# A two-layer encoder on one core: the Toeplitz blocks of the state-space branch recorded per half, and DMA prices of the list scheduler changed

## The chip, the cores and the metric

The kernel runs on one core of a Trainium2 chip. The metric is the device time of one execution in microseconds (us), lower is better. The engines are TensorE (PE in the rows; PEld is its weight load), VectorE (DVE), ScalarE (ACT), GpSimd (POOL) and SyncE (SP). SP does nothing but issue DMAs; POOL issues some too. Line L745 is the one line of the scheduler's `emit` through which every instruction of the kernel before is issued (L751 after the change), so all rows carry it, and work is told apart by the names of its tiles.

## The reference

Two layers over x of 256 tokens by 1024 channels, all float32:

```
for l in range(2):
    mod = silu(c) @ w_ada[l] + b_ada[l]            # shift, scale, gate, twice
    h = layer_norm(x) * (1 + scale1) + shift1
    proj = h @ w_in[l]                             # all branches and three gates
    o_mla = latent_attention(...); o_ret = retention(...); o_s5 = s5(s5_u, ...)
    merged = sig(g0)*(o_mla @ w0) + sig(g1)*(o_ret @ w1) + sig(g2)*(o_s5 @ w2)
    x = post_norm(ALPHA * x + gate1 * (merged @ w_o[l]))
    h = layer_norm(x) * (1 + scale2) + shift2
    x = post_norm(ALPHA * x + gate2 * conv_ffn(h))
```

The part that the change touches is `s5`: 32 groups of 16 channels, each with a complex diagonal recurrence of 64 states, run forward and backward over the tokens, whose outputs are added; then a gelu and a gated 512x512 product.

## The kernel before

**Weights.** Each weight block of 128x1024 (512 KB) is loaded as `raw` by SP, cast by ACT to a rounded `hi`, and VectorE forms `lo` = raw - hi. Every large product is three matmuls (hi by hi, lo by hi, hi by lo). Some blocks come through POOL's DMAs instead (`hd`, `ld`). The adaptive-norm weights `ada` and `adab` are loaded by SP in blocks of the same size.

**The state-space branch.** The 256 tokens are cut into 32 blocks of 8. What reaches a block from other blocks goes through the states: `U` and `w1` give `St`, scaled sums of these give `X`, and matmuls `Y<-w,X` bring it to the output. What the 8 tokens of a block do to one another is the direct term: a Toeplitz matrix of 8x8 blocks of 16x16 channels. Its 15 different blocks, 240 columns, are computed as `kps` (matmuls of `bbt` by `w`), and ACT and VectorE write them to the tile `R`, one tile for m = 0, 1 and one for m = 2, 3 (m counts four slices of the channels; the two tiles are called half 1 and half 2 here). To lay them out as a matrix, each half goes to DRAM (`rd<-R`, 4 DMAs) and comes back eight times, each time 16 columns further on (`T<-rd`, 16 DMAs of 64 KB a half, 8 for each of its two tiles `T`). Then 8 matmuls `Y<-T,U` for each m add the direct term to `Y`. Behind `Y` follow gelu, `zF`, the gated product `glu_ps`, the branch's output product `br_ps`, the output projection `wo_acc`, and the residual sum and norm (`y`, `xn`, h), before the first matmul `upt` of the feed-forward part.

**Order.** No instruction is issued where it is written. All go to a `Recorder` with their dependences, their place in the program as priority (with a small jitter), and a duration from `cost()`. `schedule()` then simulates the five engines: each free engine takes the ready instruction of best priority whose tiles find a place (tiles lie in pools of fixed size; the pool `k4` has 37 places of 4 KB a partition, and holds `raw`, `hi`, `lo`, `R` and `T`). Each engine executes the order that comes out, in that order. A DMA also waits until the one issued eight earlier by the same engine has landed. Work that may fill waits is recorded between the steps of a branch by `filler(n)`: products of the gates (`g_ps`) and of the other branches (`br_ps`), and gate weights.

**Names and lines.** `Pool` is at line 387, the duration of a DMA at 507 to 509, the transfer model of `schedule()` at 690 to 692, the loop over m of the direct term from 1754, `filler(F_S5)` at 1777, and the DRAM round trip at 1778 to 1785. In `cost()` a DMA of SP keeps its queue for 600 ns and lands 2000 ns and its bytes later, one of POOL 1100 and 2500. The round trip of both halves is recorded after the loop over m, so its priority is behind all four m and their fillers.

Of the kernel before, what the change touches and what calls it, by code (L numbers as in the profile page):

```python
# [10 lines left out]
F32 = mybir.dt.float32  # L11
# [10 lines left out]
P = 128  # L22
# [363 lines left out]

class Pool:
    def __init__(self, rec, real, bufs, psum):
        self.rec, self.real, self.bufs, self.psum = rec, real, bufs, psum

    def tile(self, shape, dt, tag=None, name=None):
        s = Slot(self.rec, self, shape, dt, tag, name)
# [22 lines left out]
class Recorder:  # L415
# [79 lines left out]
    @staticmethod  # L495
    def cost(eng, method, outs, ins, kw):
        n = max([r.free() for r in outs + ins] or [1])
        psum = any(r.tile_.pool.psum for r in outs + ins)
        if eng == "PE":
            if method == "transpose":  # L500
                return 109, 60
            n, m = kw["rhs"].free(), kw["lhsT"].free()
            if kw["rhs"].tile_.dt == F32R:
                return max(107, n / 2.4) + 13.5, 60
            t = 4 * max(n, 16) / 2.4
            return (t / 4 + 22 if m <= 32 else max(t, 4 * m / 2.4) / 2 + m / 2.4 if m <= 64 else max(t, 4 * m / 2.4) + 4), 60
        if method == "dma_start":
            by = [r for r in outs + ins]
            return (1100 if eng == "POOL" else 600), (2500 if eng == "POOL" else 2000) + sum(r.idx.shape[0] * 16 * r.free() * 4 for r in by) / 360
        if eng == "ACT":  # L510
            aps = sum(isinstance(kw.get(k), Ref) for k in ("scale", "bias"))
            return (65 if psum else 100) + 0.82 * n + 88 * aps + (93 if "accum_out" in kw else 0), 90
        aps = sum(isinstance(kw.get(k), Ref) for k in ("scalar", "scalar1", "scalar2"))
        if eng == "POOL":
            if method == "memset":
                return 60 + 0.3 * n, 90
            if kw.get("op") == ALU.pow:
                return 300 + 165 * n, 90
            if method == "tensor_scalar":
                return 175 + (0.6 if kw.get("op1") else 3.36) * n, 90  # L520
            if n < 300:
                return 200 + 1.8 * n, 90
            few = any(0 in z for r in ins for z in [np.diff(r.idx[0].ravel()[:2])])
            return 148 + (1.67 if few else 2.1) * n, 90
        if method == "tensor_tensor_scan":
            return 68 + 2.07 * n, 90
        if method == "transpose":
            return 80 + 1.94 * n, 90
        if method in ("tensor_copy", "tensor_scalar", "memset") and not psum:
            return 66 + 0.53 * n + 60 * aps, 90  # L530
        return 68 + 1.042 * n + 60 * aps, 90
# [31 lines left out]
    def schedule(self):  # L563
# [14 lines left out]
        for k, v in self.tags.items():  # L578
# [4 lines left out]
            if need[k].max(initial=0) > self.bufs[k]:  # L583
                i = int(need[k].argmax())
# [50 lines left out]
        while done < len(ops):  # L635
            progress = True
            while progress:
                progress = False
                for e in names:
# [48 lines left out]
                            ticks[k] = ticks.get(k, 0.0) + o.cols * max(0.0, min(b, k + 1) - max(a, k)) / (b - a)  # L688
                    busy[e] = now + dur
                    if o.method == "dma_start":  # L690
                        dma_free = max(dma_free, now + o.dur) + (o.lat - (2500 if e == "POOL" else 2000))
                        o.end = dma_free + (2500 if e == "POOL" else 2000)
                    else:
                        o.end = now + dur
                    heapq.heappush(events, (busy[e], -1))
# [53 lines left out]
def build(tc, A, dbg=None):  # L749
# [4 lines left out]
    def pool(name, bufs, **kw):  # L754
        return Pool(rec, ctx.enter_context(tc.tile_pool(name=name, bufs=1, **kw)), bufs, kw.get("space") == PSUM)

    cp = pool("const", 1)
    drp = pool("dram", 1, space=DRAM)
    k4 = pool("k4", N4)
    k2 = pool("k2", N2)  # L760
    k1 = pool("k1", N1)
# [16 lines left out]
    def bank(shape, name):  # L778
        return psp.tile(shape, F32, tag="ps", name=name)
# [638 lines left out]
    def mixer(l, xt, h, s5, xdram, ready=None, pre_=None):  # L1418
# [330 lines left out]

        R = [t4([P, 2, 2, 240], "R") for _ in range(2)]  # L1750
        Y = [bank([P, 4, P], "Y") for _ in range(2)]
        for m in range(4):
            w2 = [s5.gen(m, d, "w2") for d in range(2)]
            kps = [bank([P, 2, P], f"kps{g}") for g in range(2)]
# [14 lines left out]
            for d in range(2):  # L1769
                for r in range(2):  # L1770
                    with rec.group():
                        for g in range(2):
                            for qq in range(4):
                                mm(out=Y[g][32 * qq:32 * qq + 32, m], lhsT=X[d][grp[g], r, m * 4 + qq],
                                   rhs=w2[d][grp[g], r, qq].rearrange("p a b -> p (a b)"),
                                   start=(m == 0 and d == 0 and r == 0), stop=False)
            filler(F_S5)
        Tt = [t4([P, 4, 2, P], "T") for _ in range(4)]
        for mh_ in range(2):
            rd = drp.tile([16, 4, 4, 240], F32, name=f"rd{l}{mh_}")  # L1780
            for qq in range(4):
                SY.dma_start(out=rd[:, qq], in_=R[mh_][32 * qq:32 * qq + 16].rearrange("p m g x -> p (m g) x"))
            for m, i in ((m, i) for m in range(2) for i in range(8)):
                SY.dma_start(out=Tt[2 * mh_ + m][16 * i:16 * i + 16],
                             in_=rd[:, :, 2 * m:2 * m + 2, (7 - i) * 16:(7 - i) * 16 + P])
        for m in range(4):
            with rec.group():
                for g, qq in ((g, qq) for g in range(2) for qq in range(4)):
# [191 lines left out]
```

## Time and profile before

| | before |
|---|---|
| time, median of 3 runs | 1040.67 us (1039.1 to 1042.18) |
| profiled execution, its own time | 1044.28 us |
| its span | 1042.5 us |
| TensorE busy | 968.3 us (93%) |
| VectorE busy | 839.1 us (80%) |
| ScalarE busy | 516.2 us (50%) |
| GpSimd busy | 84.1 us (8%) |
| DMA | 232.98 MB, 223 GB/s on average |
| mean granted clock of TensorE | 0.984 |

The profiled execution has 1.8 us outside its span and is 3.6 us above the median of the runs. TensorE is busy in 93% of the span, so time can only be won in its 74 us of idle time or where it ran at the lower of its two clock levels. The chain of waits that ended last lies on TensorE for 69%, on VectorE for 15% and on DMAs for 7%; `T<-rd` is 2% of it.

### The profile page before, as it was taken

How to read it: one execution, taken by the hardware profiler on the slowest of the kernel's cores; microseconds unless marked ns; L12 is line 12 of the kernel's file. 1: busy time of each engine (PE TensorE's matmuls, PEld its weight loads, DVE VectorE, ACT ScalarE, POOL GpSimd, SP SyncE). 2: the span in 40 equal slices, each digit the busy share in tenths (PEclk: the TensorE clock that was granted, in tenths of full speed). 3: DMA queues.
4: the chain of work that ended last, by engine and by line, in shares of the span. 5: the costliest groups of instructions: out<-in, count | busy, mean ns of one | idle time of the engine just before them, and what ended most of it. 6: DMA issues, size and time to landing. Idle time of an engine off the chain costs nothing.

```text
span 1042.5 us, 21330 instructions
## 1 busy us (share of the span) xinstructions
PE 968.3 (93%) x8470; PEld 849.1 (81%) x8470; DVE 839.1 (80%) x1659; ACT 516.2 (50%) x895; POOL 84.1 (8%) x115
## 2 busy tenths in 40 slices
PE   4899998888998999999989999998799979999995
PEld 3689877678986799999957988687698869999994
DVE  8999998944499996777898788899266999777766
ACT  2357464224464565555635556532246466555640
POOL 0022123000002000000012010130000010000001
PEclk9999999999999999999999999999999999999998
DMA  9988589697975975555559563796898466555601
GB/s 352 408 342 183 162 220 266 153 235 249 393 269 197 355 279 196 183 189 175 184 215 396 180 170 115 175 245 149 219 388 297 145 222 206 199 182 183 221 2 41
DMA packets 72499, 232.98 MB, mean 223 GB/s; under 512 B 8384, under 2 KB 16592, under 8 KB 72400
## 3 DMA queue, kind: packets, MB, share of 16 engines
q1 hardware_dynamic: 62032, 193.88, 52.6%
q0 software_dynamic: 10368, 37.75, 15.2%
q8 instruction: 66, 1.08, 0.4%
q14 instruction: 33, 0.27, 0.1%
HBM read 228.50 MB, written 3.10 MB: 222 GB/s over the span
## 4 chain that ended last, share of the span: by engine, by line
PE 69%; DVE 15%; DMA 7%; issue 3%; ACT 2%; SPq 2%; POOL 1%; POOLq 0%; DVEq 0%; ACTq 0%
PE up_ps L745 22%; PE dn_acc L745 11%; PE g_ps L745 8%; PE b L745 6%; DVE g L745 3%; PE br_ps L745 3%; PE upt L745 3%; DMA T<-rd 2%; PE ada_ps L745 2%; SPq L745 2%; PE u_ps L745 2%; DMA raw<-in_wts 2%; PE wo_acc L745 2%; DMA hd<-in_wts 2%; DVE lo L745 2%
## 5 line engine op out<-in xcount | busy, mean ns | idle before, releaser
L745 DVE TENSOR_TENSOR lo<-raw,hi 128x1024 fp32r<-128x1024 f32 (+1 forms) x210 | 252.4, 1216 | 72.6 <-ACT hi L745 25.9
L745 ACT CAST hi<-raw 128x1024 fp32r<-128x1024 f32 (+1 forms) x210 | 214.1, 1041 | 76.1 <-DMA raw<-in_wts 27.5
L745 PE MATMUL up_ps<-hh,hi 128*128 128x256 f32 x640 | 181.2, 283 | 0.0
L745 PE MATMUL up_ps<-hlo,hi 128*128 128x256 f32 x640 | 181.1, 283 | 0.0
L745 PE MATMUL up_ps<-hh,lo 128*128 128x256 f32 x640 | 181.0, 283 | 0.0
L745 PEld LDWEIGHTS up_ps<-hh,hi 128*128 128x128 f32 x640 | 122.7, 192 | 2.5 <-issue 1.2
L745 PEld LDWEIGHTS up_ps<-hlo,hi 128*128 128x128 f32 x640 | 122.7, 192 | 1.6 <-issue 0.4
L745 PEld LDWEIGHTS up_ps<-hh,lo 128*128 128x128 f32 x640 | 122.7, 192 | 0.1
L745 DVE SCALAR_TENSOR_TENSOR cv<-up_ps,small,cv 128x255 f32<-128x255 f32 x176 | 73.0, 477 | 14.8 <-ACT cv L745 14.8
L745 PE MATMUL g_ps<-hh,hd 128*128 128x256 f32 x256 | 77.2, 301 | 1.0 <-ACT pe L745 1.0
L745 PE MATMUL g_ps<-hlo,hd 128*128 128x256 f32 x256 | 74.6, 292 | 0.0
L745 PE MATMUL g_ps<-hh,ld 128*128 128x256 f32 x256 | 74.2, 290 | 0.0
L745 PE MATMUL dn_acc<-lo,ah 128*128 128x512 f32 x176 | 68.4, 392 | 0.0
L745 PE MATMUL dn_acc<-hi,ah 128*128 128x512 f32 x176 | 66.7, 392 | 0.0
L745 PE MATMUL dn_acc<-hi,al 128*128 128x512 f32 x176 | 66.3, 390 | 0.0
L745 ACT ACTIVATE cv<-up_ps,small 128x256 f32<-128x256 f32 x88 | 44.6, 561 | 34.5 <-PE up_ps L745 34.3
L745 ACT ACTIVATE gt<-g_ps 128x256 f32<-128x256 f32 x48 | 18.2, 382 | 79.6 <-PE g_ps L745 79.6
L745 ACT ACTIVATE ld<-hd 128x1024 fp32r<-128x1024 f32 x36 | 37.9, 1062 | 35.2 <-DMA hd<-in_wts 24.2
L745 PEld LDWEIGHTS g_ps<-hh,hd 128*128 128x128 f32 x256 | 49.8, 195 | 5.8 <-issue 3.7
L745 PEld LDWEIGHTS g_ps<-hh,ld 128*128 128x128 f32 x256 | 49.8, 195 | 1.2 <-issue 1.1
L745 PEld LDWEIGHTS g_ps<-hlo,hd 128*128 128x128 f32 x256 | 49.8, 194 | 1.2 <-issue 0.8
L745 ACT CAST hl<-raw 128x512 fp32r<-128x512 f32 x48 | 29.0, 620 | 42.6 <-PE br_ps L745 12.2
(332 smaller groups left out, 2329.9 us busy)
## 6 DMA issues: line engine op xcount, KB each, us to landing
raw<-in_wts SPq DMA_DIRECT2D x226, 512.0 KB, 4.9
ada<-in_wts SPq DMA_DIRECT2D x48, 512.0 KB, 8.9
adab<-in_wts SPq DMA_DIRECT2D x48, 512.0 KB, 10.2
hd<-in_wts POOLq DMA_DIRECT2D x36, 512.0 KB, 6.8
ld<-in_wts POOLq DMA_DIRECT2D x36, 512.0 KB, 7.8
T<-rd SPq DMA_DIRECT2D x64, 64.0 KB, 4.6
lnrow<-in_rows SPq DMA_DIRECT2D x8, 512.0 KB, 8.7
raw<-in_wts SPq DMA_DIRECT2D x8, 416.0 KB
```

What stands on the lines that cost most here:

```text
L745: getattr(o.eng.real, method)(*a, **kw)
```

## The change

The DRAM round trip becomes a function, `toeplitz`, which is recorded inside the loop over m, for half 1 after m = 1 and for half 2 after m = 3, each ahead of that m's filler; so it gets an earlier priority. The `T` tiles are asked for there, too. And `cost()` prices DMAs anew: POOL 800 ns of queue and 4500 ns and the bytes; SP where it reads a DRAM tile of the program's own 620 and 4600 without bytes; every other DMA of SP 380 and 2000 and the bytes. The prices are used only by the scheduler's simulation.

```diff
 class Pool:
     def __init__(self, rec, real, bufs, psum):
-        self.rec, self.real, self.bufs, self.psum = rec, real, bufs, psum
+        self.rec, self.real, self.bufs, self.psum, self.dram = rec, real, bufs, psum, False
...
         if method == "dma_start":
-            by = [r for r in outs + ins]
-            return (1100 if eng == "POOL" else 600), (2500 if eng == "POOL" else 2000) + sum(r.idx.shape[0] * 16 * r.free() * 4 for r in by) / 360
+
+            by = sum(r.idx.shape[0] * 16 * r.free() * 4 for r in outs + ins) / 360
+            if eng == "POOL":
+                return 800, 4500 + by
+            if any(r.tile_.pool.dram for r in ins):
+                return 620, 4600
+            return 380, 2000 + by
...
                     if o.method == "dma_start":
-                        dma_free = max(dma_free, now + o.dur) + (o.lat - (2500 if e == "POOL" else 2000))
-                        o.end = dma_free + (2500 if e == "POOL" else 2000)
+                        fix = 4500 if e == "POOL" else 4600 if o.lat == 4600 else 2000
+                        dma_free = max(dma_free, now + o.dur) + (o.lat - fix)
+                        o.end = dma_free + fix
...
+    drp.dram = True
...
+        Tt = []
+
+        def toeplitz(mh_):
+
+            rd = drp.tile([16, 4, 4, 240], F32, name=f"rd{l}{mh_}")
+            for qq in range(4):
+                SY.dma_start(out=rd[:, qq], in_=R[mh_][32 * qq:32 * qq + 16].rearrange("p m g x -> p (m g) x"))
+            for m in range(2):
+                Tt.append(t4([P, 4, 2, P], "T"))
+                for i in range(8):
+                    SY.dma_start(out=Tt[-1][16 * i:16 * i + 16], in_=rd[:, :, 2 * m:2 * m + 2, (7 - i) * 16:(7 - i) * 16 + P])
+
         for m in range(4):
...
+            if m % 2:
+                toeplitz(m // 2)
             filler(F_S5)
-        Tt = [t4([P, 4, 2, P], "T") for _ in range(4)]
-        for mh_ in range(2):
...
```

No engine gets more or other work, but for one copy that goes from ACT to VectorE (1659 and 1660 instructions on VectorE, 854 and 853 in the order of ACT). The order changes on every engine and over the whole program, since every load has a new price. Three places follow.

The first is SP's queue in layer 1, around the two round trips; `rd_8684` is half 1, `rd_8982` (after the change `rd_9024`) half 2. Before:

```order
L745 DMA rd_8684<-R 16x960 x4
L745 DMA T<-rd_8684 16x8x128 x16
L745 DMA rd_8982<-R 16x960 x4
L745 DMA ada<-in_wts 128x1024 x2
L745 DMA raw<-in_wts 128x1024 x2
L745 DMA T<-rd_8982 16x8x128 x16
```

and after the change:

```order
L751 DMA rd_8684<-R 16x960 x4
L751 DMA T<-rd_8684 16x8x128 x16
L751 DMA rows<-in_rows 128x1024
L751 DMA raw<-in_wts 128x1024 x2
L751 DMA rd_9024<-R 16x960 x4
L751 DMA raw<-in_wts 128x1024 x3
L751 DMA adab<-in_wts 128x1024 x3
L751 DMA T<-rd_9024 16x8x128 x16
```

Three loads moved between half 1's return and half 2's way out, and six instead of four stand ahead of half 2's return. In layer 0 five loads (three `ada`, two `raw`) stand in the first gap, where there was none, and four (three `raw`, one `rows`) in the second, where there were five. On TensorE, where in layer 0 three matmuls stood between the `Y<-T,U` of m = 0 and of m = 1, the two now stand back to back, with 47 matmuls of fillers between the last `kps` and the first of them (39 before), and 31 between the third and fourth (16 before). In layer 1, 132 matmuls stand between the second and the third (73 before).

The second place is VectorE's queue in the front of layer 0, ahead of the rotated keys `kr` (whose branch, like `uT` behind it, TensorE's order waits for there). Before:

```order
L745 SCALAR_TENSOR_TENSOR gtmp<-gtmp 128x16
L745 TENSOR_TENSOR lo<-raw,hi 128x1024
L745 CAST hh<-hf 128x2x128
L745 TENSOR_TENSOR hlo<-hf,hh 128x2x128
L745 TENSOR_TENSOR lo<-raw,hi 128x1024
L745 TENSOR_SCALAR ve<-ss 128x1
L745 TENSOR_TENSOR rot_85<-g_799,g_808 128x32x16
L745 TENSOR_SCALAR ve<-ss 128x1
L745 TENSOR_TENSOR kr<-b_310,cst 128x16
```

and after the change:

```order
L751 CAST hh<-hf 128x2x128
L751 SCALAR_TENSOR_TENSOR gtmp<-gtmp 128x16
L751 TENSOR_TENSOR hlo<-hf,hh 128x2x128
L751 SCALAR_TENSOR_TENSOR lg<-gtmp 128x16
L751 CAST hh<-hf 128x2x128
L751 TENSOR_SCALAR nlg<-lg 128x16
L751 TENSOR_TENSOR hlo<-hf,hh 128x2x128
L751 TENSOR_TENSOR w_899<-g_853,g_867 128x512
L751 TENSOR_TENSOR g_904<-pw,bbt 128x512
L751 TENSOR_TENSOR lo<-raw,hi 128x1024
L751 TENSOR_SCALAR ve<-ss 128x1 x2
L751 TENSOR_TENSOR kr<-b_312,cst 128x16
```

In all, 16 more instructions stand ahead of `kr` (278 instead of 262): ten small ones of the retention decays (`gtmp`, `lg`, `nlg`), four products `g<-pw,bbt`, one `w` and one `lo`; ahead of `uT` it is 17 more. On TensorE 33 `g_ps` matmuls that stood among those of `w_ps` and `St` right behind this place now come later.

The third place is VectorE's queue at the end of layer 0's mixer, where the residual sum `y` starts the norm on which the feed-forward part waits. Before:

```order
L745 TENSOR_TENSOR lo<-raw,hi 128x1024
L745 TENSOR_TENSOR bbt<-g_3938,g_3945 128x32x16
L745 TENSOR_TENSOR lo<-raw,hi 128x1024
L745 TENSOR_TENSOR g_4128<-rot_4111,rot_538 128x32
L745 TENSOR_TENSOR y<-wo_acc,rows 128x512 x2
L745 TENSOR_TENSOR y<-y,xa 128x512
```

and after the change:

```order
L751 TENSOR_TENSOR g_4173<-rot_3981,rot_540 128x32x4
L751 TENSOR_TENSOR rot_4051<-g_4173,g_4178 128x32x4
L751 TENSOR_TENSOR g_4194<-rot_4051,rot_540 128x32x8
L751 TENSOR_TENSOR rot_3981<-g_4188,g_4194 128x32x8
L751 TENSOR_TENSOR y<-wo_acc,rows 128x512 x2
L751 TENSOR_TENSOR g_4188<-rot_3981,rot_540 128x32x8
L751 TENSOR_TENSOR y<-y,xa 128x512
```

Twenty small products of the next layer's rotation tables (`rot`, `g`), which stood behind `y`, now stand ahead of it.

## Rows read from the trace of the kernel before

**Rows 1.** Waits of TensorE: us in total, times, longest.

```profile
PE Y L745 <- DMA T<-rd: 10.3, 5, 3.0
...
PE Y L745 <- issue: 1.6, 1, 1.6
```

**Rows 2.** Timeline of TensorE, direct term, layer 0: start, length, idle before.

```profile
222.66 0.64 PE L745 MATMUL Y<-T,U 128*32 128x128 f32 x16
...
226.84 0.65 PE L745 MATMUL Y<-T,U 128*32 128x128 f32 x16 [2.99 <-DMA T<-rd]
...
246.91 0.65 PE L745 MATMUL Y<-T,U 128*32 128x128 f32 x16 [1.71 <-DMA T<-rd]
```

**Rows 3.** Timeline of TensorE, direct term, layer 1.

```profile
733.47 0.64 PE L745 MATMUL Y<-T,U 128*32 128x128 f32 x16 [1.35 <-DMA T<-rd]
...
746.96 0.65 PE L745 MATMUL Y<-T,U 128*32 128x128 f32 x16 [2.03 <-DMA T<-rd]
...
752.27 0.64 PE L745 MATMUL Y<-T,U 128*32 128x128 f32 x16 [2.20 <-DMA T<-rd]
```

**Rows 4.** Windows: length, then busy time of PE, PEld, DVE, ACT, POOL; clock; DMA.

```profile
227.70:231.10 3.40, 3.40 (x18) 3.40 (x18) 0.00 (x0) 0.00 (x0) 0.00 (x0) 0.50 0.88 300
753.40:756.80 3.40, 3.40 (x18) 3.40 (x17) 2.25 (x3) 3.40 (x6) 0.00 (x0) 0.50 1.03 414
```

**Rows 5.** Timeline of SP's DMA issues, layer 0: start, stretch, count.

```profile
202.35 1.73 SPq L745 DMA_DIRECT2D rd<-R  x4
207.61 14.73 SPq L745 DMA_DIRECT2D T<-rd  x16
222.45 2.04 SPq L745 DMA_DIRECT2D rd<-R  x4
...
226.49 1.78 SPq L745 DMA_DIRECT2D raw<-in_wts  x4
228.49 16.38 SPq L745 DMA_DIRECT2D T<-rd  x16
```

**Rows 6.** Waits of SP's queue, 205 to 246 us.

```profile
SPq L745 <- DMA raw<-in_wts: 5.0, 4, 1.7
...
SPq L745 <- DVE g L745: 2.4, 1, 2.4
```

**Rows 7.** Timeline of SP's DMA issues, layer 1.

```profile
730.50 3.38 SPq L745 DMA_DIRECT2D rd<-R  x4
...
737.46 12.72 SPq L745 DMA_DIRECT2D T<-rd  x16
```

**Rows 8.** Timeline of VectorE, the writes that complete the two halves of R, layer 0.

```profile
201.99 0.30 DVE L745 TENSOR_TENSOR R<-R,kps 128x16 f32<-128x16 f32 x2
...
219.28 0.17 DVE L745 TENSOR_TENSOR R<-R,kps 128x16 f32<-128x16 f32 x1
```

**Rows 9.** Windows of four stages, columns as in rows 4.

```profile
50.00:105.00 55.00, 54.76 (x481) 47.77 (x479) 52.74 (x118) 35.37 (x65) 11.76 (x17) 1.00 0.85 264
165.00:219.00 54.00, 46.26 (x797) 37.92 (x796) 50.47 (x118) 17.05 (x39) 9.78 (x13) 1.00 0.77 195
322.00:338.00 16.00, 12.44 (x105) 8.96 (x104) 15.61 (x30) 7.38 (x14) 5.58 (x5) 0.97 0.71 273
755.00:800.00 45.00, 45.00 (x384) 43.02 (x384) 27.49 (x33) 24.51 (x38) 0.00 (x0) 0.98 0.96 361
```

**Rows 10.** VectorE's work by shape, 21 to 100 us: count, busy, mean ns, idle before.

```profile
L745 DVE TENSOR_TENSOR lo<-raw,hi 128x1024 fp32r<-128x1024 f32 x14 | 16.8, 1221 | 0.3 <-ACT hi L745 0.2
L745 DVE TENSOR_TENSOR g<-pw,bbt 128x512 f32<-128x512 f32 x10 | 6.5, 675 | 0.0
...
L745 DVE SCALAR_TENSOR_TENSOR gtmp<-gtmp 128x16 f32<-128x16 f32 x9 | 1.4, 159 | 0.0
```

**Rows 11.** Timeline of VectorE ahead of layer 0's first residual sum.

```profile
322.00 0.21 DVE L745 TENSOR_TENSOR g<-rot,rot 128x32 f32<-128x32 f32 x1
322.19 1.29 DVE L745 TENSOR_TENSOR y<-wo_acc,rows 128x512 f32<-128x512 f32 x2
```

More of the change, by code (lines that the diff above doesn't have):

```diff
@@ L1776, in mixer @@
                                    start=(m == 0 and d == 0 and r == 0), stop=False)
+            if m % 2:
+                toeplitz(m // 2)
             filler(F_S5)
-        Tt = [t4([P, 4, 2, P], "T") for _ in range(4)]
-        for mh_ in range(2):
[L1780 to L1785, printed above, removed]
         for m in range(4):
```

## The prediction

> **What bounds the kernel now.** I read the busy times first: TensorE works for 968 of 1042.5 us, so its idle time and its stretches at the lower clock are all there is to win, and anything that adds idle time to it is lost. Then the waits of TensorE by tile: for the direct term it waits 10.3 us in five waits for `T<-rd`, and once 1.6 us that end in "issue" [rows 1]. The timeline gives each wait's place: in layer 0 none before m = 0, 2.99 us before m = 1, 1.58 before m = 2 (the issue wait of rows 1) and 1.71 before m = 3 [rows 2]; in layer 1 1.35, 2.03 and 2.20 [rows 3]. That is 6.28 and 5.58 us, together 11.9. Last, the windows: three such waits are followed by a stretch of 3.4 us in which TensorE was busy throughout and the granted clock was 0.50, the 1.2 GHz level; rows 4 show two of the three, the other begins at 248.2. At half clock 3.4 us do 1.7 us of work, so these cost 5.1 us more. All in all 17.0 us hang on the arrival of `T`.
>
> What sets that arrival: half 1 is complete at 202.29 (201.99 and 0.30) [rows 8], and its DMAs to DRAM are issued from 202.35 [rows 5], at once. So the earlier priority can win nothing ahead of half 1. Its sixteen returns then hold SP for 14.7 us (207.61 to 222.34) [rows 5], 2.4 of them in one wait for VectorE to give a place in the pool [rows 6]. Half 2 is complete at 219.45 [rows 8], but goes out from 222.45 [rows 5], 3.0 us late, since the queue is still issuing half 1's returns. In layer 1 it is alike: half 2's way out starts at 730.50 and the return at 737.46 [rows 7].
>
> **The change part by part.** The profiled execution, 1044.28 us, is what the sum is made against; the median of the runs is 3.6 us below it.
>
> *Layer 0, half 1.* The ninth return of half 1 no longer stands behind a tile that VectorE must free, which took 2.4 us [rows 6]; the second `T` lands by so much earlier. On TensorE m = 0 and 1 stand together behind eight more matmuls of filler. Full-clock filler takes 0.12 us a matmul (384 in 45.00 us) [rows 9], so TensorE also comes 1.0 us later, less the three matmuls, 0.36 us, that were between. The wait of 2.99 us thus shrinks by 2.4 at least and vanishes at most: I take -2.4. The stretch at half clock right behind it [rows 4] goes if the pause does: -1.7.
>
> *Layer 0, half 2.* Five loads stand newly ahead of its way out. Four `raw` issue in 1.78 us [rows 5], 0.45 each, so 2.2 us, which eats the 2.4 that half 1 gave; its return stands behind four loads instead of five. I take -0.4 for the one issue fewer; bounds are -3.3 (both waits gone) and +4, for the case that the loads' data hold up the returns: four waits for `raw` cost 5.0 us in this place already [rows 6].
>
> *Layer 1.* TensorE has 59 more matmuls between m = 1 and m = 2 (132 and 73), 49 of which are net over the stretch from half 1 to the last `Y<-T,U`: 5.9 us of cover. Against it half 2's way out stands behind three loads, at 0.45 us 1.3 us, and its return behind two more than before, 0.9 us by their issue and 2.9 by their data (512 KB at 361 GB/s is 1.45 us each) [rows 9]. So of 5.58 us of waits 1.9 to 3.9 should be left; I take 2.5, -3.1, and half a chance that the stretch at half clock from 753.4 [rows 4] goes: -0.9. The filler taken forward is missing after `Y`: TensorE is busy 45.00 of 45 us from 755 to 800 [rows 9], so 5.9 us less there cost nothing while the gelu and the product behind it arrive within the 39 us that are left; if they didn't, up to 5.9 us would come back.
>
> *Front of layer 0.* Ahead of `kr` VectorE gets ten small operations of 0.159 us, five of the 128x512 kind of 0.675 and one `lo` of 1.22 [rows 10]: 6.2 us by their lengths, about 5.1 to 5.7 since one starts before the one ahead ends. From 50 to 105 us TensorE has 0.24 us of idle time, VectorE 2.3 [rows 9]. So TensorE's order, which now has 33 filler matmuls (4.0 us) fewer among `w_ps` and `St`, waits there for `kr` and `uT`. It is not lost in full: the work is only moved, VectorE's queue up to the completion of R is 1 us longer and no more, and TensorE has 7.7 us of idle time from 165 to 219 [rows 9] which the deferred filler can take. Bounds 0 and +5.7; I take +3.0, in the middle, for want of a row that is nearer.
>
> *End of layer 0's mixer.* Twenty small products of 0.21 us, starting 0.19 after one another [rows 11], move ahead of `y`: 4.0 us, less what moves behind it, 2.9 net. `y` started directly behind the operation ahead of it [rows 11], and VectorE is busy 15.61 of 16 us while TensorE waits 3.6 of them [rows 9]. So nothing hides VectorE's work but what `wo_acc` still lacks then; bounds 0 and +2.9; I take +2.0.
>
> *All the rest* (the FFN, the other boundaries, layer 1's front) keeps its order to within some tenths, and I take nothing for it; the copy that goes to VectorE is under 0.7 us on an engine with slack.
>
> The sum: -2.4 - 1.7 - 0.4 - 3.1 - 0.9 + 3.0 + 2.0 = -3.5, so 1040.8 for a profiled execution and 1037.2 on the scale of the median.
>
> One rule speaks against the gain. In the rows SP's waits for `raw` sit in the middle of half 2's returns, four of them [rows 6]: loads issued ahead of small returns do hold them up. The Trainium skill's page "DMA: Bandwidth & Descriptors", section "Queues, rings and completion order", says the same from below: on each DMA engine the descriptors of one issuing engine's row are consumed in ring order. By it, two more loads ahead of the return in layer 1 would cost their full data time (the 2.9 above and not the 0.9), and the sum would be about 2 us worse; the trace agrees in direction and shows no size for it alone.
>
> **The rivals.**
>
> *A. The front of layer 0 decides (slower).* VectorE's 5.7 us ahead of `uT` become 5.7 us of TensorE idle time that nothing gives back, since VectorE paces this part anyway (52.74 of 55 us, 50.47 of 54) [rows 9], and `y` comes 2.9 late; of the gain the 4.1 of layer 0's half 1 remains: +5.7 + 2.9 - 4.1 = +4.5, 1045.2. For it: no idle time there that could hide anything. Against: the idle time from 165 on. It decides once more than 4 of the 8.6 us stay.
>
> *B. The loads eat the gain.* Layer 0's half 1 keeps its 4.1, but half 2 arrives as late as TensorE does, in both layers (no -0.4, -3.1, -0.9): +0.9, 1041.6. For it: five and three loads in the way of half 2, three and six more ahead of returns [rows 6]. Against: the 49 matmuls of cover.
>
> *C. VectorE's moves are absorbed.* Deferred filler takes the idle time from 165 to 219, and `y` waits for `wo_acc` in any case: -8.5, 1032.2. At the far end all 17.0 us go: 1023.7.
>
> *D. Nothing changes for T,* since half 1 was sent at once before [rows 5, 8] and half 2 waits behind the same queue: the waits stay, the two costs are small: 1040.7.
>
> **How the numbers follow.** A measurement of this kernel can tell a change of about 0.3%, 3.1 us. I give the forecast (1033.5 to 1040.5) 0.33, of which 0.23 lies below 1037.5; A 0.24, C 0.20, B 0.14, D 0.09. Faster: 0.23 + 0.20 = 0.43. Same: 0.10 of the forecast, nearly all of B and D and a little of A: 0.31. Slower: 0.22 of A and 0.04 of B, 0.26. The range for 8 in 10 leaves a tenth on each side: below it most of C's far part, above it the full price of A with a stretch at half clock more: 1029 to 1046. The forecast's own range is 1033.5 to 1040.5.
>
> **What would show it.** In layer 0 m = 0 and 1 of `Y<-T,U` stand together with a wait under 0.6 us, and no window at clock 0.50 follows. In layer 1 the waits before `Y<-T,U` add up to 2 to 4 us instead of 5.58. From 50 to 105 us TensorE shows 2 to 6 us of idle time that ends with `kr`, `uT` or `w_ps` and VectorE, and its idle time from 165 to 219 is smaller by about half of that. `y` starts 2 to 3 us later against the end of `wo_acc`. The prediction is wrong if TensorE's idle time changes mainly elsewhere, if half 2's returns land over 4 us later against the completion of R, or if the front keeps its 0.24 us.

## The result, and the profile after

The changed kernel takes 1050.78 us (median of 4 runs, 1049.38 to 1051.92), the one before 1040.72 beside it: a ratio of 1.0085 with an interval of 1.0062 to 1.0109. It is slower by 10 us, where 3.5 us less were forecast, and lies above the stated range. The two profiled executions, which the rest of this section compares, differ by 7.6 us (1051.92 and 1044.28).

The page of the changed kernel, its span, the busy times and the granted clock in 40 slices:

```profile
span 1049.9 us, 21329 instructions
...
PE 974.5 (93%) x8470; PEld 855.7 (81%) x8470; DVE 841.4 (80%) x1660; ACT 517.7 (49%) x894; POOL 84.3 (8%) x115
...
PEclk8989999998999899999999999999899989999998
```

TensorE is busy 974.5 us with the same 8470 matmuls that took 968.3 before: 6.2 us of the 7.4 by which the two spans differ. Its idle time grew by 1.2 us only (75.4 and 74.2). So most of the difference between the two profiles is busy time, which the same matmuls spend where TensorE runs at 1.2 GHz. The waits of TensorE (us in total, times, longest):

```profile
PE Y L751 <- DMA T<-rd: 17.7, 4, 6.0
...
PE ada_ps L751 <- DMA adab<-in_wts: 8.5, 3, 4.7
...
PE h_ps L751 <- DVE gtmp L751: 2.3, 1, 2.3
```

The waits for `T` are 17.7 us and not the forecast 6 [rows 1]; the other two rows had 3.7 us (for `adab`) and nothing of that kind before. On the timeline the `Y<-T,U` stand as the order had them, but wait longer [rows 2, 3]:

```profile
222.93 0.65 PE L751 MATMUL Y<-T,U 128*32 128x128 f32 x16
...
228.04 0.92 PE L751 MATMUL Y<-T,U 128*32 128x128 f32 x16 [4.47 <-DMA T<-rd]
...
248.18 1.08 PE L751 MATMUL Y<-T,U 128*32 128x128 f32 x16 [5.64 <-DMA T<-rd]
...
733.63 0.64 PE L751 MATMUL Y<-T,U 128*32 128x128 f32 x16
...
740.72 1.08 PE L751 MATMUL Y<-T,U 128*32 128x128 f32 x16 [6.01 <-DMA T<-rd]
...
764.95 0.65 PE L751 MATMUL Y<-T,U 128*32 128x128 f32 x16 [1.61 <-DMA T<-rd]
```

In layer 1 the first of them started before the change at

```profile
731.48 0.65 PE L745 MATMUL Y<-T,U 128*32 128x128 f32 x16
```

These starts tell where the time goes, since as many matmuls, to within two, stand ahead of them in both kernels. At the first `Y<-T,U` of layer 0 the changed kernel is 0.3 us behind (222.93 and 222.66); from there to the last `dn_acc`, the end of layer 0's feed-forward part, it loses 4.6 us, wins 2.7 in the front of layer 1, and loses 5.2 us from layer 1's first `Y<-T,U` on. The loss lies behind `Y<-T,U`, in both layers.

At two of these waits, and elsewhere, the windows (columns as in rows 4) show stretches at 0.50 that last 6.8 us, where each was 3.4 [rows 4]. There are seven of 6.8 us in this execution ahead of its end. One of them is at a wait for VectorE's `gtmp` and two are at waits for `T`:

```profile
67.80:74.60 6.80, 6.53 (x25) 5.13 (x18) 5.68 (x20) 3.48 (x10) 0.52 (x1) 0.50 0.32 125
245.30:252.10 6.80, 3.92 (x29) 3.57 (x30) 0.00 (x0) 1.01 (x2) 0.00 (x0) 0.50 0.48 101
736.90:743.70 6.80, 2.98 (x25) 2.63 (x26) 0.00 (x0) 1.06 (x1) 0.84 (x1) 0.50 1.04 322
```

Three others (340.9, 651.5 and 842.7 us) have 3.4 us near their place in the kernel before. The seventh, at 20.1 us, stood there before too: the clock record of that execution begins only at 26.3 us, but the same matmul takes 0.55 us at 21 us in both kernels, before (first line; the second is at full clock) and after (third line). So the mean clock of 0.984 before counts some 6 us at half clock as full.

```profile
21.34 0.55 PE L745 MATMUL b<-lo,hh 128*128 128x416 f32 x1
40.18 0.35 PE L745 MATMUL b<-lo,hh 128*128 128x416 f32 x1
...
21.17 0.55 PE L751 MATMUL b<-lo,hh 128*128 128x416 f32 x1
```

What made `T` late is in SP's issues: layer 0 in full, then half 2 of layer 1 [rows 5, 7]:

```profile
204.68 12.59 SPq L751 DMA_DIRECT2D T<-rd  x16
217.38 2.22 SPq L751 DMA_DIRECT2D ada<-in_wts  x3
219.70 4.47 SPq L751 DMA_DIRECT2D raw<-in_wts  x2
225.52 3.82 SPq L751 DMA_DIRECT2D rd<-R  x4
230.37 5.34 SPq L751 DMA_DIRECT2D raw<-in_wts  x3
236.70 0.33 SPq L751 DMA_DIRECT2D rows<-in_rows  x1
237.40 12.82 SPq L751 DMA_DIRECT2D T<-rd  x16
...
733.04 7.54 SPq L751 DMA_DIRECT2D rd<-R  x4
...
747.75 15.08 SPq L751 DMA_DIRECT2D T<-rd  x16
```

and in VectorE's last write to R, layer 0 and layer 1 [rows 8]:

```profile
219.10 0.29 DVE L751 TENSOR_TENSOR R<-R,kps 128x16 f32<-128x16 f32 x2
...
732.53 0.17 DVE L751 TENSOR_TENSOR R<-R,kps 128x16 f32<-128x16 f32 x1
```

R's half 2 is complete at 219.39, as before, but its way out is issued from 225.52 to 229.34 and its return from 237.40; before it was 222.45 to 224.49 and 228.49. In layer 1 the way out starts 0.3 us behind R (732.70), but takes 7.5 us for four DMAs, and the return starts at 747.75. A DMA of SP waits for the landing of the one issued eight earlier. For the ways out that was mostly not a load but one of half 1's own last returns; so SP's queue waited 6.8 us for `T` in layer 0 (the second `raw` and the first two ways out) and 6.0 in layer 1 (the ways out):

```profile
SPq L751 <- DMA T<-rd: 6.8, 3, 3.7
...
SPq L751 <- DMA T<-rd: 6.0, 2, 4.2
```

Behind the ways out the loads wait for earlier loads, in layer 0 3.0 us for `ada` and 3.0 for `raw` between 230 and 237.4 us, and half 2's return stands behind them. Read off T's 512-byte packets in the trace, half 2 has landed 50.4 and 50.9 us after R's half 1 was complete, 43.9 and 41.3 before.

Half 1's returns, for which the ways out waited, landed late themselves. In layer 0 the last of them was issued at 216.65, 4.0 us earlier than before, and its last packet moved at 227.43, 1.1 us later. In that stretch the DMA engines are busy without a gap, at 256 GB/s (clock, DMA share and GB/s are the last three columns):

```profile
216.65:227.43 10.78, 6.92 (x101) 6.32 (x83) 3.58 (x10) 4.03 (x9) 1.69 (x2) 1.00 1.09 256
```

In it SP issued five loads of 512 KB, of which 1.2 loads' worth of bytes moved, and GpSimd's queue moved 3.4. In layer 1 the last return landed 9.5 us after its issue, beside 2.9 loads' worth from GpSimd and 1.2 from SP; in layer 0 of e10 below, with no load moving, it took 2.0 us. The Trainium skill, page "DMA: Bandwidth & Descriptors", section "Queues, rings and completion order", says that each DMA engine takes turns between the queue rows it has work for, a whole packet from one before the next. The late tail beside GpSimd's loads agrees with that; no run here measures it alone.

The front of layer 0, 50 to 105 us and 165 to 219 us [rows 9]:

```profile
50.00:105.00 55.00, 52.03 (x391) 45.50 (x392) 52.35 (x115) 35.41 (x64) 10.78 (x16) 0.94 0.77 249
165.00:219.00 54.00, 49.79 (x841) 41.62 (x837) 51.27 (x119) 18.14 (x42) 11.07 (x14) 1.00 0.79 198
```

TensorE's idle time there is 2.97 us instead of 0.24, and 4.21 instead of 7.74.

### The profile page after: what moved, and what is told of

Its sections match the earlier page's. It is cut to its first block, busy times and chain, and to the rows that moved or that the text cites. A ratio compares the mean times of both kernels' runs of the same rounds, so it can differ in the third digit from the quotient of the medians.

```text
span 1049.9 us, 21329 instructions
## 1 busy us (share of the span) xinstructions
PE 974.5 (93%) x8470; PEld 855.7 (81%) x8470; DVE 841.4 (80%) x1660; ACT 517.7 (49%) x894; POOL 84.3 (8%) x115
## 5 line engine op out<-in xcount | busy, mean ns | idle before, releaser
L751 PE MATMUL g_ps<-hlo,hd 128*128 128x256 f32 x256 | 74.2, 290 | 0.0
L751 ACT ACTIVATE cv<-up_ps,small 128x256 f32<-128x256 f32 x88 | 44.9, 562 | 30.8 <-PE up_ps L751 30.3
L751 DVE TENSOR_TENSOR hl<-raw,hl 128x512 fp32r<-128x512 f32 x48 | 32.1, 684 | 32.7 <-ACT hl L751 32.5
```

Of the source, the lines that this page charges most:

```text
L751: getattr(o.eng.real, method)(*a, **kw)
```

## The experiments

A short name for each edit: *move* is the round trip recorded inside the loop over m; *SP 380*, *POOL* and *T* are the three new prices. The seed is that of the scheduler's jitter. "Fillers" counts the matmuls that the order puts on TensorE between the `Y<-T,U` of half 1 and the first of half 2, in layer 0 and layer 1, repeats counted (on this count the kernel before has 93 and 84, where the text above counts rows for layer 1). "Waits" is TensorE's time before `Y<-T,U` in the profiled execution, unless VectorE ended it. The ratio is to the kernel before on the same chip.

| kernel | median us | ratio, interval | waits us | fillers |
|---|---|---|---|---|
| before | 1040.7 to 1044.1 | 1 | 11.9 | 93, 84 |
| whole change | 1050.8 | 1.0085, 1.0062 to 1.0109 | 17.7 | 97, 149 |
| e1 move | 1037.7 | 0.9941, 0.9921 to 0.9961 | 7.0 | 151, 160 |
| e2 the three prices, no move | 1051.4 | 1.0076, 1.0048 to 1.0105 | 11.3 | 73, 71 |
| e3 before, seed 18 | 1038.1 | 0.9950, 0.9929 to 0.9972 | 10.3 | 144, 145 |
| e4 whole change, seed 18 | 1052.5 | 1.0091, 1.0066 to 1.0116 | 17.3 | 144, 152 |
| e5 move, SP 380 | 1045.7 | 1.0042, 1.0022 to 1.0061 | 13.3 | 140, 147 |
| e6 move, POOL | 1033.6 | 0.9926, 0.9904 to 0.9947 | 9.6 | 177, 175 |
| e7 move, T | 1049.0 | 1.0066, 1.0035 to 1.0098 | 16.6 | 144, 140 |
| e8 move, POOL, T | 1044.9 | 1.0030, 1.0002 to 1.0058 | 12.4 | 171, 145 |
| e9 whole change, T not behind rd | 1047.2 | 1.0046, 1.0028 to 1.0064 | 16.7 | 97, 149 |
| e10 move, T with bytes | 1029.9 | 0.9880, 0.9851 to 0.9910 | 7.0 | 172, 172 |
| e11 move, T without bytes, 2364 | 1053.0 | 1.0102, 1.0071 to 1.0133 | 17.3 | 127, 124 |
| e12 move, POOL, SP 900 | 1039.7 | 0.9964, 0.9944 to 0.9984 | 3.8 | 100, 109 |
| e13 e10 with Y of half 2 earlier | 1049.6 | 1.0078, 1.0049 to 1.0107 | 16.7 | 127, 124 |
| e14 whole change, T with bytes | 1042.0 | 1.0002, 0.9978 to 1.0026 | 10.9 | 132, 176 |
| e15 move, POOL, T with bytes | 1037.9 | 0.9956, 0.9934 to 0.9977 | 9.1 | 199, 176 |
| e16 e10, seed 18 | 1034.6 | 0.9928, 0.9904 to 0.9952 | 6.7 | 172, 161 |
| e17 e11, seed 18 | 1049.2 | 1.0054, 1.0037 to 1.0071 | 17.7 | 151, 128 |
| e18 e10 with 7000 | 1034.2 | 0.9901, 0.9874 to 0.9929 | 0.7 | 192, 201 |

Every kernel with more than 12 us of these waits is slower than the one before, every one with less than 10.5 is faster; between them lie e2, which is slower, e14, which is the same, and the kernel before itself.

### The two halves of the change, and another seed

e1 takes the diff without its prices, e2 its prices without the move; e3 and e4 change one line:

```diff
-JITTER = (17, 2)
+JITTER = (18, 2)
```

> The round trip recorded inside the loop over m, with the old DMA prices. In SP's order 3 loads stand ahead of half 2's way out and 6 ahead of its return in layer 0, 5 and 7 in layer 1 (before the change 0 and 5, 0 and 4; with the whole change 5 and 4, 3 and 6). Queue theory (the loads that SP issues ahead of half 2 and GpSimd's loads make T late, and the waits bring stretches at half clock): as slow as the whole change or slower, 1049 to 1057 us, waits of TensorE for T<-rd over 17 us. Price theory (the new prices make worse orders everywhere, the move is harmless): 1038 to 1043. Draw theory (the order before is a lucky one of many, any rearrangement loses it): 1045 to 1055, whatever the loads.

> The new DMA prices, with the round trip recorded behind the loop over m as before. In SP's order 3 loads stand ahead of half 2's way out and 2 ahead of its return in layer 0, 0 and 4 in layer 1. Queue theory: layer 1 as before, layer 0 a little late, 1040 to 1046, waits for T<-rd 8 to 13 us. Price theory: as slow as the whole change, 1049 to 1053. Draw theory: 1045 to 1055.

> The kernel before with the seed of the scheduler's jitter at 18 instead of 17, nothing else. In SP's order 4 loads stand ahead of half 2's way out and 5 ahead of its return in layer 0, 1 and 9 in layer 1. Queue theory: T late in both layers, 1048 to 1056, waits for T<-rd over 17 us. Price theory: 1039 to 1043, since the prices are the old ones. Draw theory: 1045 to 1055.

> The whole change with seed 18. 6 loads ahead of half 2's way out and 6 ahead of its return in layer 0, 6 and 7 in layer 1, more than with seed 17. Queue theory: slower than the changed kernel, 1052 to 1058. Price theory: the same as the changed kernel within 3 us, 1048 to 1054. Draw theory: anything from 1045 to 1055, with no relation to the loads.

The move alone is a gain (0.9941), the prices alone are the whole loss (1.0076). The queue theory, which was the cause I had in mind, falls: e1 has 21 loads ahead of half 2's ways out and returns and e3 has 19, the whole change 18, and both are faster than the kernel before. The draw theory falls as well: with the old prices another seed is faster, with the new ones it is as slow as the first. The price theory is left; e1 and e3 come out 0.3 and 0.9 us below its ranges.

### One price at a time

Each adds one price to e1, e8 two. The edits are the three cases of `cost()`, with the fixed part in `schedule()`'s transfer model to match:

```diff
             if eng == "POOL":
-                return 1100, 2500 + by
+                return 800, 4500 + by              # e6, e8
+            if any(r.tile_.pool.dram for r in ins):
+                return 620, 4600                   # e7, e8
-            return 600, 2000 + by
+            return 380, 2000 + by                  # e5
```

> The move with one of the three new prices: 380 instead of 600 ns of SP's queue for an ordinary DMA; GpSimd's price and the price of reads of T as before. If this price makes the loss (loads packed more densely into SP's order from the front on): 1046 to 1053 us, and 1035 to 1041 for the three others but the ones that have it. If GpSimd's price or that of T makes it: 1035 to 1041 here. If no single price does and each adds a part: 1040 to 1043.

> The move with GpSimd's new price alone (800 and 4500 ns instead of 1100 and 2500). If this price makes the loss: 1046 to 1053 us. If SP's 380 or the price of T makes it: 1035 to 1041. If each adds a part: 1040 to 1043.

> The move with the new price for SP's reads of the program's own DRAM tiles alone (620 and 4600 ns without bytes instead of 600, 2000 and the bytes). If this price makes the loss: 1046 to 1053 us. If SP's 380 or GpSimd's price makes it: 1035 to 1041. If each adds a part: 1040 to 1043.

> The move with GpSimd's price and the price of T's reads, without SP's 380, so the whole change less that one number. If SP's 380 makes the loss: 1035 to 1041 us. If one of the two others makes it: 1046 to 1053. If each adds a part: 1043 to 1047.

No single price is alone to blame: T's adds 1.25% to the move (1.0066 against 0.9941), SP's 380 adds 1.0%, GpSimd's takes 0.15% away, which the intervals don't tell from nothing. The sum is more than the whole change shows (they would give 1.015), so the two losses overlap.

SP's 380 shows in the trace from the front on. Up to the first `w_ps` of layer 0, e1 (first row) and e5 have the same 672 matmuls, but VectorE has 13 more instructions and 5.8 us more work ahead, and the place is reached 5.0 us later:

```profile
0.00:95.51 95.51, 78.84 (x672) 64.63 (x673) 88.97 (x326) 44.97 (x85) 14.13 (x26) 0.98 0.94 339
...
0.00:100.54 100.54, 79.98 (x672) 66.26 (x673) 94.75 (x339) 45.40 (x85) 12.95 (x26) 0.97 0.88 321
```

2.1 of the 5.0 us are given back by the first `Y<-T,U` (219.4 and 222.3 us). The larger part, 5.1 us, comes from layer 1's first `Y<-T,U` on, where e5 waits 6.2 us for `xn`, the norm ahead of the feed-forward part (e1 1.2):

```profile
PE h_ps L749 <- ACT xn L749: 6.2, 1, 6.2
```

The whole change has no such wait (2.1 us), so what 380 costs there was not taken apart.

### What in the price of T

```diff
-            return 620, 4600          # e7
+            return 620, 4600 + by     # e10
+            return 620, 2364          # e11
```

e9 keeps the changed kernel's order and lets the reads of T take another source at the moment of issue, which leaves out the direct term's values; e12 puts SP's price at 900 instead of 600, with GpSimd's new price.

> The changed kernel with its order kept to the instruction, but the 64 DMAs that fill T read equally shaped rows of the input x instead of rd (left out: the direct term's values, which are then not those of the reference). They still stand in their places in SP's order, behind the way out of their half and the loads, but no longer wait for the way out to land. If the late T is what costs (TensorE's waits of 17.7 us for it and the stretches at half clock behind them): T comes 2 to 4 us earlier a half, waits for T 8 to 12 us, 1042 to 1047 us. If the loss lies elsewhere in the new order: 1049 to 1052.

> The move, and of the price of T's reads the later landing alone: 620 and 4600 ns and the bytes (the change prices them without bytes); the rest as before the change. If the free bytes are what hurts (the scheduler believes that 64 reads of T take no DMA time): 1035 to 1041 us, as the move alone. If the 4600 ns are what hurts: 1045 to 1051.

> The move, and of the price of T's reads the missing bytes alone: 620 and 2364 ns (where the bytes made 2364 before) without occupying the scheduler's model of the DMA engines. If the free bytes are what hurts: 1045 to 1051 us. If the 4600 ns are what hurts: 1035 to 1041.

> The move, GpSimd's new price, the price of T's reads as before the change, and 900 ns of SP's queue for every DMA of SP, the other direction from 380. In SP's order no load stands ahead of half 2's way out and 3 ahead of its return in layer 0. If cheap DMAs in the scheduler's model make orders that count on data too early (optimism theory), a dearer one does no harm or helps: 1028 to 1036 us. If 600 is merely the value that the order was fitted to and any other loses: 1040 to 1047.

e10 and e11 part the two halves of T's price: the later landing with the bytes gives 1029.9 us, the fastest kernel here, the missing bytes 1053.0, the slowest. With e1 and e7 they make a square: with the bytes the ratio is 0.9941 at 2000 ns (e1) and 0.9880 at 4600, without them 1.0102 at 2364 and 1.0066 at 4600 (e7). So the missing bytes cost 1.6 and 1.9%; the later landing gains 0.6 and 0.4%, the second not told from nothing. e9 gains 0.4% on the changed kernel by the ratios, at the edge of both expectations, and its waits go from 17.7 to 16.7 only, where 8 to 12 were expected: the wait for `rd` to land is a small part. e12 lies between its two expectations: faster than the kernel before, but slower than e6, which has 600 in its place. Dearer is not better by itself, against the optimism theory in its simple form.

The traces of e10 and e11 show how the bytes act. They agree to 0.4 us up to the first `Y<-T,U` (219.26 and 219.63). From the first to the last one, layer 0 and layer 1, TensorE's busy time is the first number behind the length, e10:

```profile
219.26:248.54 29.28, 25.81 (x268) 23.21 (x268) 4.92 (x10) 6.21 (x12) 0.85 (x1) 1.00 0.82 247
715.93:747.28 31.35, 27.86 (x270) 24.98 (x270) 5.40 (x12) 6.20 (x12) 1.71 (x2) 0.95 0.89 250
...
PE Y L751 <- DMA T<-rd: 3.9, 3, 1.8
PE Y L751 <- issue: 3.1, 1, 3.1
...
243.70 0.64 PE L751 MATMUL Y<-T,U 128*32 128x128 f32 x16 [1.75 <-DMA T<-rd]
248.17 0.64 PE L751 MATMUL Y<-T,U 128*32 128x128 f32 x16 [1.72 <-DMA T<-rd]
743.77 0.65 PE L751 MATMUL Y<-T,U 128*32 128x128 f32 x16
746.91 0.64 PE L751 MATMUL Y<-T,U 128*32 128x128 f32 x16 [0.38 <-DMA T<-rd]
```

and e11:

```profile
219.63:250.58 30.95, 21.46 (x210) 19.27 (x210) 4.91 (x9) 5.48 (x9) 0.87 (x1) 0.82 0.83 235
735.40:764.86 29.46, 21.70 (x209) 19.13 (x209) 5.41 (x10) 5.60 (x9) 0.00 (x0) 0.83 0.86 272
...
PE Y L751 <- DMA T<-rd: 17.3, 4, 8.6
...
245.33 1.08 PE L751 MATMUL Y<-T,U 128*32 128x128 f32 x16 [8.63 <-DMA T<-rd]
249.92 1.08 PE L751 MATMUL Y<-T,U 128*32 128x128 f32 x16 [0.86 <-DMA T<-rd]
759.46 1.08 PE L751 MATMUL Y<-T,U 128*32 128x128 f32 x16 [6.75 <-DMA T<-rd]
764.20 1.08 PE L751 MATMUL Y<-T,U 128*32 128x128 f32 x16 [1.01 <-DMA T<-rd]
```

T lands at about the same time: the last `Y<-T,U` of layer 0 start 28.9 and 30.3 us behind the first. But e10 has 268 matmuls to do in the stretch and e11 210, so e11 waits 17.3 us, and its clock falls to 0.82 and 0.83 of full, against 1.00 and 0.95. In `schedule()` a DMA's bytes push back `dma_free`, and with it the end of every later DMA. Sixteen reads at 364 ns are 5.8 us a half; without them the model believes that T arrives that much earlier when the DMAs are the limit, so it finds `Y<-T,U` ready while there is still filler, and TensorE's order has it too early. The 4600 ns of the change give only 2.2 of that back. Of the 25.1 us by which the two spans differ, 14.3 lie between the first `Y<-T,U` and the end of layer 0 and 5.6 from layer 1's first `Y<-T,U` on; 4.8 lie in the front of layer 1, where no run says why. Nor are the reads free: in a stretch of the kernel before that holds nothing but such reads, the DMA engines are 39% busy (the last columns are clock, DMA share, GB/s):

```profile
240.00:244.00 4.00, 2.42 (x32) 2.05 (x31) 0.87 (x1) 0.00 (x0) 0.00 (x0) 1.00 0.39 94
```

94 GB/s for 4 us are 5.7 reads of 64 KB, so one takes 0.39 * 4 / 5.7 = 0.27 us of all the DMA engines.

### The place of Y alone, and the best prices

e13 takes e10's order and moves the four groups, as many matmuls earlier as they stand in e11:

```diff
     rec.plan()
+    for half, back in ((1, (45, 50)), (3, (48, 53))):
+        for o, n in zip(adds[2 * half:2 * half + 2], back):
+            at = ...               # n matmuls of TensorE ahead of o
+            lst.remove(o); lst.insert(at, o)
     rec.emit(tc)
```

e14 is the diff with `+ by` behind its 4600, e15 is e10 with GpSimd's new price, e16 and e17 are e10 and e11 with seed 18, e18 has `return 620, 7000 + by`.

> The order of the fast kernel of 1029.9 us (the move, T's reads late and with bytes), with nothing changed but the place of Y<-T,U of half 2 in TensorE's order: in each layer they stand as many filler matmuls earlier as in the order of the kernel of 1053 us (127 and 11 behind the first pair in layer 0, 124 and 11 in layer 1, instead of 172 and 16, and 172 and 16). Place theory (the price acts by putting these matmuls ahead of filler that could have covered the wait): TensorE's waits for T rise from 3.9 us to 14 to 18, and the time to 1042 to 1055 us. If the price acts through the rest of the order: 1029 to 1034.

> The whole change, except that the price of T's reads keeps its bytes (620, 4600 and the bytes). Fillers between the pair of half 1 and the first of half 2: 132 in layer 0 and 176 in layer 1 (97 and 149 in the changed kernel, 172 and 172 in the fast one). Place theory: between the two, 1036 to 1043 us, SP's 380 making the rest. If the 380 ns or the sum of the prices outweigh it: 1046 to 1052.

> The move, GpSimd's new price and the price of T's reads at 620 and 4600 with the bytes; SP's other DMAs at 600. 199 and 176 fillers ahead of half 2's Y<-T,U. If GpSimd's price gives here too what it gave to the move alone (4 us): 1023 to 1028 us. If the waits for T that it saved are gone already: 1028 to 1033.

> The fast kernel of 1029.9 us with seed 18 of the scheduler's jitter: 172 and 161 fillers ahead of half 2's Y<-T,U. Place theory: 1029 to 1037 us, near the other seed and below the kernel before. Draw theory (1029.9 was one lucky order): 1038 to 1050.

> The move and T's reads at 620 and 2364 without bytes, with seed 18: 151 and 128 fillers ahead of half 2's Y<-T,U, against 172 and 161 with the bytes and 4600 at the same seed (1034.6 us). Place theory: 1043 to 1053 us, waits for T over 12 us. Draw theory (the 23 us between the two prices at seed 17 were two draws): 1030 to 1042.

> The move and T's reads at 620, 7000 and the bytes, seed 17: 192 and 201 fillers ahead of half 2's Y<-T,U (172 and 172 at 4600). Place theory: the waits for T, 3.9 us at 4600, go to under 2 us, and the time stays at 1027 to 1032 us, since little is left to win and the work behind Y starts later. If the place decides by itself, the further the better: 1020 to 1026. If 4600 was a lucky order: 1035 to 1045.

e13 takes 1049.6 us against e10's 1029.9, with nothing moved but these four groups: the place theory holds (by the ratios, 1.0078 and 0.9880, the step is 2.0%). Its profile, taken in the fastest of its executions (1041.6 us; the other five lie between 1049.0 and 1050.3), shows the two stretches with 211 and 209 matmuls and waits near those of e11:

```profile
219.34:247.58 28.24, 21.17 (x211) 19.01 (x210) 3.74 (x8) 3.51 (x7) 0.85 (x1) 0.88 0.87 254
722.47:753.33 30.86, 21.21 (x209) 18.75 (x209) 5.40 (x12) 4.15 (x8) 1.71 (x2) 0.89 0.89 248
...
PE Y L751 <- DMA T<-rd: 14.5, 4, 6.5
PE Y L751 <- issue: 2.2, 1, 2.2
```

In this execution the span is 12.5 us longer than e10's, 10.7 of it idle time; 6.6 us of it lie between the first `Y<-T,U` and the end of layer 0, 6.0 from layer 1's first `Y<-T,U` on, and nothing elsewhere. The other five ran at a lower clock (0.970 on average, e10 0.981), so the rest up to 19.7 us goes along with a lower clock; their traces were not taken, so its cause is not shown.

e14 mends the change's loss by one term: 1.0002 instead of 1.0085. Its trace is the closest answer to the changed kernel's: T arrives as late (50.6 and 50.4 us behind R's half 1, the last return of half 1 in layer 0 again 10.6 us after its issue), but 132 and 176 fillers instead of 97 and 149 stand ahead, and the waits are 10.9 us instead of 17.7. What is left against e10 is SP's 380 and GpSimd's price together. e15 shows that GpSimd's price, which did the move alone no harm, does some here: 0.9956 against 0.9880, slower than both expectations; why is open. e16 and e17 repeat the contrast at the other seed, 0.9928 against 1.0054: of the 2.2% at seed 17, 1.3% are there again, so part of e10's 1029.9 was its draw. e18 takes the waits to 0.7 us and is not faster than e10, between its expectations of 1027 to 1032 and 1035 to 1045: beyond 172 fillers nothing more was had.

Open stays why e2 loses: its waits for T are no longer than before, yet it is as slow as the whole change, so the place theory does not account for it. It shares the late front with e5 (first `w_ps` at 100.6 us), but has made that good by the first `Y<-T,U`, which starts at 220.5 us, 2.2 earlier than before. From there to the end of layer 0 it loses 3.6 us, in the front of layer 1 1.5, and from layer 1's first `Y<-T,U` on 4.0, where it waits for `xn` as e5 does:

```profile
PE h_ps L751 <- ACT xn L751: 7.2, 2, 6.6
```

Its idle time in all is that of the kernel before (74.0 and 74.2 us); the same matmuls are busy 7.3 us longer (975.6). So it loses by the clock, and no run says what brings that.

## Why the prediction was wrong

The step that failed is the arrival of half 2, in "Layer 0, half 2" and "Layer 1": a size, and a wait that was left out. I let a load ahead of half 2 cost its issue, 0.45 us, or its data, 1.45, and came to -0.4 and to 2.2 to 4.2 us later. Measured is an arrival 6.5 and 9.6 us later, by R's half 1; 1.1 and 2.5 of that is R's half 2 itself, which is complete so much later behind half 1, and the rest, 5.4 and 7.0 us, is past the 4 us that the prediction named as a sign that it is wrong. What the sum has no term for is that half 2's ways out wait for half 1's own returns to land, and that these land late beside loads: SP's queue stood 6.8 and 6.0 us for them. The cover in layer 1 was more than counted: TensorE's busy time between the first and the last `Y<-T,U` grew from 15.6 to 24.1 us, where 5.9 were forecast; in layer 0 only four matmuls more stand ahead of half 2. The delay was larger in both. So the waits went from 6.28 to 10.11 us and from 5.58 to 7.62, together +5.9 where -5.9 was forecast. Rival B had this mechanism at 1041.6 and with too small a size.

But a late arrival alone does not decide, as e1, e3, e10 and e14 show: T comes 48 to 51 us behind R's half 1 there, too, and none of them is slower than the kernel before. What I never asked is what the prices make the scheduler believe. The diff shows that T's reads lose their bytes; I read it as the model's matter and looked only at the order that came out, without asking whether `Y<-T,U` stands where T would be. That layer 0 has 97 fillers, four more than before, while five loads move ahead of half 2's way out, was to be seen in the order before the run. That `Y<-T,U` stands too early is shown by moving it (e13, in e10's order) and by the bytes alone (e14); the changed kernel with nothing but its `Y<-T,U` moved later was not run.

*Layer 0, half 1* (-2.4): the wait for a place in the pool went, as forecast, and the last return was issued 4.0 us earlier; the wait is 4.47 us instead of 2.99, since the last return landed 10.8 us after its issue among loads. Wrong, +1.5.

*The clock* (-2.6): nothing of it came. At the waits of 5.6 and 6.0 us stand 6.8 us at 0.50, behind that of 4.5 us 3.4 us, as before behind waits of 2 to 3 us. But TensorE is busy for only 3.92 and 2.98 us of the two long ones, so at half of its busy time the three stretches at T cost 5.2 us, as against 5.1 before. The 6.2 us more of busy time come from other places, for which the sum had no term: I counted stretches that would go, and none that would come. The front has one of 6.8 us where it had none, there are 3.4 us more at each of 340.9, 651.5 and 842.7 us, and a new one of 3.4 us at 856.3. Apart from the front, no run says what brings them.

*Front of layer 0* (+3.0): the idle time came as said, 2.97 us, and a stretch at half clock with it: behind the wait of 2.3 us for VectorE's `gtmp` stand 6.8 us with TensorE busy for 6.53, some 3.3 us of work put off. Both were given back by the first `Y<-T,U`, which starts 0.3 us later than before, so the term is +0.3 and rival A is not there. By e5, SP's 380 makes the front late (5.0 us at the first `w_ps`).

*End of layer 0's mixer* (+2.0): `y` starts 3.4 us ahead of the end of `wo_acc` instead of 7.0, later than forecast, but it was not paid: what TensorE waits for there now is `adab`, 4.7 us, and the idle time from the last `Y<-T,U` to the first `upt` is 4.9 us (5.2 before).

Idle time outside the direct term fell by 4.7 us, where +5.0 was forecast, so that the 5.9 us more of waits for `T` and the 6.2 us more of busy time come to 7.4 us of span.

## What to carry to other kernels

A list scheduler with an in-order emission did better here with the arrival of slow data priced late rather than early: where its model has a transfer come too soon, the consumer is put ahead of the filler that should have covered it, and the engine stands. When a price in such a model is replaced, keep every resource that the transfer occupies (here the bytes, 5.8 us a half) before the latency is mended, and compare the consumer's place in the order with the arrival in the trace. And change one price at a time: here two lost, one did nothing that could be told, and the move that came with them was worth 0.6%.

## What the runs showed of the hardware

A read of 64 KB from DRAM in runs of 512 bytes takes 0.27 us of all DMA engines at 94 GB/s when alone. The last of 16 such reads landed 2.0 us after its issue with no load moving (e10, layer 0), 5.7 in the kernel before and 10.8 in the changed kernel, among 4.5 loads' worth of bytes. In this program a DMA of SP stands behind the landing of the one issued eight earlier, so in layer 1 four DMAs of 60 KB took 7.5 us to issue. The time of one kernel moves with the granted clock from one execution to the next: e13's six lie between 1041.6 us (mean granted clock 0.976) and 1050.3 us (0.970 on average in the other five). And the clock record of an execution may begin some us behind its first matmuls (26.3 us before the change, TensorE's first matmul at 10.8), so that its mean clock comes out too high.
